# Scaling the sample states on ScalarE and adding a PSUM bank at once, in a PE-bound decoder step

## The chip, the cores and the metric

One Trainium2 chip, one of its cores. The metric is the device time of one launch in microseconds (us). Each run comes with a profile of one execution: a page of sums and a trace of every instruction. PE is TensorE's matmul side, PEld its weight loads, DVE is VectorE, ACT is ScalarE, POOL is GpSimd, SP is the sync engine, which here only issues DMAs.

## The reference

One inference step of a two-layer hybrid decoder trunk with D_MODEL = 1024: a prompt of 512 tokens, and 8 samples of 4 tokens each that continue from stored states. Layer 0 has an mLSTM/GLA mixer and an MLP, layer 1 a Mamba-2 SSD mixer and an MLP. The change is in the SSD mixer, and there in what becomes of the samples' states. Cut to that:

```python
def _ssd_chunk(h0, inp):
    x, Bm, Cm, dt, a = inp                      # L = 4 tokens for a sample
    cs = jnp.cumsum(a, axis=1)
    ...
    y = y + jnp.einsum('btgn,bgrpn->btgrp', Cm, h0) * jnp.exp(cs)[..., None]
    csL = cs[:, -1]
    wL = jnp.exp(csL[:, None] - cs) * dt
    h = jnp.exp(csL)[..., None, None] * h0 + jnp.einsum('bsgr,bsgrp,bsgn->bgrpn', wL, x, Bm)
    return h, y
```

So each sample's new state h is the old one h0 times a decay for each of 32 heads, plus a product of x and Bm. There are 4 groups of 8 heads, head dimension 64, state dimension 128: for a group and a sample the state is 512 rows by 128.

## The kernel before, in words

Everything is float32; each dense product is made of three matmuls in a reduced form of float32 (high by high, high by low, low by high), 128x128 weights against 272 tokens, at L367. The tokens (512 + 32 = 544) are taken in two halves.

TensorE's order is written out by hand. The dense matmuls are its main stream. Every other piece of work is a generator in a lane (`launch(gen, lane)`): `dense` calls `tick()` before each of its matmuls, a lane counts such ticks down, and at zero its generator runs on to its next `yield n`, where n is the ticks to wait from there. `need(key)` makes a lane wait until another has marked that key as ready. The order on the other engines is made by a planner from priorities (order in the program, with some instructions raised) and its own estimate of times. Each engine, and each engine's DMA queue with it, then runs its own list in order: an instruction that waits holds what stands behind it. ScalarE (`S`), GpSimd (`G`) and SP (`nc.sync`) issue DMAs.

PSUM has three banks for the dense products (`psd`), four for everything else (`pm(...)`, called by the name of what is put in) and one kept for the samples' outputs (`it`).

The SSD stage goes over the four groups. For a group it runs the dense products of x, B and C, each followed by a convolution over time: ScalarE copies the PSUM bank into `ci` (L1472, L1475, L1477), VectorE runs the three taps `acc` (L1487), and so on. Then `group(g, Bf, Cf)` is launched, which goes over four blocks b of 128 prompt tokens and a fifth of the 32 sample tokens: `scores(b)` loads the cumulated decays from two small DRAM tensors, `d_cs` into `E` (L1524) and, for b = 1, 2, 3, `d_ecs` (their exponentials, written at L1431) into `ec` (L1529), transposes x (`xt`, L1532) and multiplies C by B (`cb`, L1534); `state(b)` updates the prompt's state `hT`; `outputs(b)` makes the outputs. `ec` has two buffers.

When a group is done it launches `samples(g, ...)` in a lane of its own: four steps of two samples (q = 0, 2, 4, 6). A step asks for the old states twice, as `h0` (transposed, for the outputs `it`, four buffers of one sample) and as `h0n` (`hn`, two buffers of two samples, 512 KB each, L1633), makes the masked `Bm` on ScalarE (L1636), and yields. Then come the matmuls: `it` (L1640) and four products into two `sps` banks (L1647). VectorE scales a 128x128 piece of the old state by its decay and adds the product from PSUM in one operation (L1653, eight in a step, four for each bank). GpSimd's queue stores the new states from the same buffer (L1654). There are 4 groups x 4 steps = 16 steps.

The weights come through `WeightStream`: a DMA into `wraw` (three buffers), a cast on ScalarE (`whi`, L166) and the rest on VectorE (`wlo`, L167), with five sets of buffers ahead of TensorE. After its convolutions a group is gated: `zt` (L1666, L1669) and its squares.

Of the kernel before, what the change touches and what calls it, by code (L numbers as in the profile page):

```python
# [9 lines left out]
F32 = mybir.dt.float32  # L10
# [3 lines left out]
ALU = mybir.AluOpType  # L14
# [3 lines left out]
P = 128  # L18
# [3 lines left out]
NB, LS = 8, 4  # L22
# [12 lines left out]
W = dict(dec=12, gates=30, gr=8, sc=16, lev=14, v=24, kd=10, out=38, ss=40, end=12, c0=20, u=13, s=16, ml=12, mr=40, dt=238, sg=72, sx=14, sq=26, so=48, l0=12, l1=12, v0=74, v1=55, f0=16, f1=18)  # L35
# [192 lines left out]
def trunk_kernel(ctx, tc, a, stages=("ab", "mlp0", "ssd", "mlp1")):  # L228
    nc = tc.nc
    V, S, G, TE = nc.vector, nc.scalar, nc.gpsimd, nc.tensor  # L230
# [6 lines left out]
    def pm(name):  # L237
        turn[0] += 1
        k = spare[0] and turn[0] % 5 == 0
        return psm.tile([P, 512], F32, tag="k" if k else "m", name=name, bufs=1 if k else 4)  # L240
# [10 lines left out]
    for st in stages:  # L251
# [10 lines left out]
        else:  # L262
# [3 lines left out]
            for kind, m, *r in MLP:  # L266
                if kind == "pair":
                    ws.plan(st, "pair", a["mlp_w1"][l, m], a["mlp_w1"][l, m + 1])
                else:
                    k, n = m % 8, r[0]  # L270
# [53 lines left out]
    def need(*keys):  # L324
        while not ready.issuperset(keys):
            yield 0
# [1029 lines left out]
    def ssd(pool, ypool, dram, right, ahead, consts):  # L1356
# [21 lines left out]
        decs = pool.tile([P, 16, NB], F32, name="decs", bufs=1)  # L1378
        d_cs = dram.tile([32, T], F32, name="d_cs")
        d_ecs = dram.tile([32, T], F32, name="d_ecs")  # L1380
# [118 lines left out]
        def group(g, Bf, Cf):  # L1499
# [6 lines left out]
            p = pm("Btp")  # L1506
# [3 lines left out]
            p = pm("Bts")  # L1510
# [4 lines left out]
            def scores(b):  # L1515

                n = P if b < 4 else NS
                tk = slice(b * P, b * P + n)
                if b < 4:
                    E = tls[b] = pool.tile([P, 8, P], F32, tag="E", name="E", bufs=2)  # L1520
                else:
                    tls[b] = pool.tile([P, 8, NS], F32, tag="E4", name="E4", bufs=1)
                    E = tls[b][:NS]
                S.dma_start(out=E, in_=d_cs[heads, tk][None].broadcast_to([n, 8, n]))  # L1524
                ec = None
                if b in (1, 2, 3):
                    ec = pool.tile([P, 4, P], F32, tag="ec", name="ec", bufs=2)
                    for e in range(2):
                        S.dma_start(out=ec[64 * e:64 * e + 64], in_=d_ecs[8 * g + e:8 * g + 8:2, tk][None].broadcast_to([64, 4, n]))  # L1529
                p = pm("xt")  # L1530
                for j in range(4):
                    TE.transpose(p[:n, j * P:(j + 1) * P], X[:, j, tk], ident)  # L1532
                c = pm("cb")
                TE.matmul(c[:n, :n], Bf[:, tk], Cf[:, tk], start=True, stop=True)  # L1534
                if b < 4:
                    z = pool.tile([P, 512], F32, tag="z", name="z", bufs=2)
                else:
                    z = pool.tile([P, 512], F32, tag="z4", name="z4", bufs=1)
                    G.memset(z[NS:2 * NS], 0.0)
                xw = pool.tile([P, 512], F32, tag="xw", name="xw", bufs=2)  # L1540
                for o, k in ((z, 0), (xw, 32)):
                    V.tensor_tensor(o[:n].rearrange("p (h c) -> p h c", h=8), p[:n].rearrange("p (h c) -> p h c", h=8),
                                    cols[:n, b, k + 8 * g:k + 8 + 8 * g, None].broadcast_to([n, 8, 64]), ALU.mult)
                cb = pool.tile([P, P], F32, tag="cb", name="cb", bufs=1)
                if b < 4:
                    S.copy(cb, c[:, :P])
                    G.affine_select(out=E, in_=E, pattern=[[0, 8], [1, P]], compare_op=ALU.is_ge, fill=-BIG,
                                    base=0, channel_multiplier=-1)
                else:
                    V.tensor_tensor(cb[:n, :n], c[:n, :n], smask[:NS], ALU.mult)  # L1550
                    V.tensor_tensor(E, E, csp[:, heads, None].broadcast_to([n, 8, n]), ALU.min)
                for r in range(8):
                    S.activation(E[:, r], E[:, r], AF.Exp, bias=ncs[:n, b, 8 * g + r:8 * g + r + 1])
                V.tensor_tensor(E, E, cb[:n, None, :n].broadcast_to([n, 8, n]), ALU.mult)
                if b == 4:
                    G.memset(tls[b][NS:2 * NS], 0.0)
                    G.tensor_copy(tls[b][64:], seye[64:, None, :].broadcast_to([64, 8, NS]))
                tls[b] = tls[b], ec, z, xw

            def state(b):  # L1560

                E, ec, z, xw = tls[b]
                tk = slice(b * P, b * P + P)
                hT = states[0]
                if b > 0:
                    ip = pm("ip")
                    for j in range(4):
                        TE.matmul(ip[:, j * P:(j + 1) * P], hT[:, j * P:(j + 1) * P], Cf[:, tk], start=True, stop=True)  # L1568
                    V.tensor_tensor(ec, ec, ip.rearrange("p (j t) -> p j t", j=4), ALU.mult)
                sp = pm("sp")  # L1570
                TE.matmul(sp, Bt[:, b], xw, start=True, stop=True)  # L1571
                hn = pool.tile([P, 512], F32, tag="hT", name="hT", bufs=2)
                if b == 0:
                    S.copy(hn, sp)
                else:
                    G.tensor_tensor(hn.rearrange("p (h c) -> p h c", h=8), hT.rearrange("p (h c) -> p h c", h=8),
                                    dec[:, heads, b:b + 1].broadcast_to([P, 8, 64]), ALU.mult)
                    V.tensor_tensor(hn, hn, sp, ALU.add)
                states[0] = hn
                if b == 3:  # L1580
                    nc.sync.dma_start(out=a["p_h"][g], in_=hn)
# [20 lines left out]
            for b in range(4):  # L1602
                state(b)
                yield W["sx"]
                if b == 3 and g > 0:
                    yield from need(("Y", g - 1))
                scores(b + 1)
                yield W["sx"]
                outputs(b)
                yield W["sx"]  # L1610
# [10 lines left out]
            S.copy(Cm.rearrange("p (q r) -> p q r", r=NS + LS)[:, :, :LS], Cf[:, NP:].rearrange("p (q l) -> p q l", l=LS))  # L1621
            launch(samples(g, X, outputs, tls[4][2], Bs, Xs), "smp")

        def samples(g, X, outputs, z, Bs, Xs):

            heads = slice(8 * g, 8 * g + 8)
            it = psm.tile([P, 512], F32, tag="k", name="it", bufs=1)
            for q in range(0, NB, 2):
                h0 = [pool.tile([P, 512], F32, tag="h0", name="h0", bufs=4) for _ in range(2)]
                for k in range(2):  # L1630
                    nc.sync.dma_start(out=h0[k], in_=a["h0"][g, q + k])
                hn = pool.tile([P, 2, 512], F32, tag="h0n", name="h0n", bufs=2)
                nc.sync.dma_start(out=hn, in_=a["h0n"][g, q // 2])  # L1633
                Bm = pool.tile([96, 2, P], F32R, tag="Bm", name="Bm", bufs=2)
                for k in range(2):
                    S.activation(Bm[:, k], Bs.bitcast(F32), AF.Identity, scale=seqm[:96, q + k:q + k + 1])  # L1636
                yield W["sq"]

                for k in range(2):
                    TE.matmul(it[64 + NS * k:64 + NS * k + NS], Cm[:, NS * (q + k):NS * (q + k) + NS], h0[k],  # L1640
                              start=q == 0, stop=q == NB - 2)
                for i in range(2):
                    sp = pm("sps")
                    spv = sp.rearrange("p (j k n) -> p j k n", j=2, k=2)
                    for j in range(2):
                        m = 2 * i + j
                        TE.matmul(sp[:, 256 * j:256 * j + 256], Xs[:, m * P:(m + 1) * P], Bm.rearrange("p k n -> p (k n)"),  # L1647
                                  start=True, stop=True)
                    for j in range(2):
                        m = 2 * i + j  # L1650
                        for k in range(2):
                            h = hn[:, k, m * P:(m + 1) * P]
                            V.scalar_tensor_tensor(h, h, decs[:, 4 * g + m, q + k:q + k + 1], spv[:, j, k], ALU.mult, ALU.add)  # L1653
                nc.gpsimd.dma_start(out=a["s_h"][g, q // 2], in_=hn)  # L1654
            V.tensor_tensor(z[64:].rearrange("p (h c) -> p h c", h=8), it[64:].rearrange("p (h c) -> p h c", h=8),
                            ecs[64:, heads, None].broadcast_to([64, 8, 64]), ALU.mult)
            yield W["so"]
            outputs(4)
            ready.add(("Y", g))
# [163 lines left out]
    n = 0  # L1823
    spill, ahead = a["xT"], None
    left = ctx.enter_context(ExitStack())
    while n < len(stages):
        st = stages[n]
        src = spill
        with ExitStack() as stk:
            if st == "ssd":  # L1830
# [5 lines left out]
                with tc.tile_pool(name="ssd", bufs=1, reuse_waits="tile") as pool:  # L1836
# [4 lines left out]
                    with tc.manual_schedule(engines={mybir.EngineType.PE}):  # L1841
                        out = ssd(pool, ypool, dram, right, ahead, consts)
# [170 lines left out]
```

## Time and profile before

| what | value |
|---|---|
| median of 3 runs | 1509.25 us (1504.87 to 1512.08) |
| the profiled execution's own time | 1500.13 us |
| its span, first to last instruction | 1498.4 us |
| PE busy | 1471.6 us, 98% of the span |
| PEld busy | 1422.7 us, 95% |
| DVE busy | 1095.3 us, 73% |
| ACT busy | 794.1 us, 53% |
| POOL busy | 227.8 us, 15% |
| mean granted TensorE clock | 0.998 |

The page gives sums over the whole execution; an engine at 73% of the span can be full in one stage. The stretch that the change touches lies between about 660 and 1000 us of the span. A line of a waits view has who waited, for whom, then the total in us, the number of waits and the longest. A line of a timeline has the start in us, the length in us, engine, line, operation, what is written and read, the shape, and in brackets the engine's idle time before it and what ended that. "ACTq" or "SPq" is an engine's queue, where it issues a DMA; the length is that of the issue, not of the transfer.

### The profile page before, as it was taken

The numbers are of one execution on the slowest core, as the hardware profiler recorded it, in microseconds if no ns is written. First come the engines' busy times: TensorE is split into PE (matmuls) and PEld (weight loads), VectorE is DVE, ScalarE is ACT, GpSimd is POOL, SyncE is SP. The second block draws the span as 40 slices with busy tenths as digits, with TensorE's granted clock in tenths as the row PEclk, the third lists the DMA queues.
The fourth block names the chain that finished last, engine by engine and source line by source line (L and its number), as shares of the span: only waits on it lengthen the run. The fifth ranks groups of instructions, "written<-read, shape, count | busy, mean of one in ns | idle before, by whom it ended". The sixth has DMA issues, their size and how long they took to land.

```text
span 1498.4 us, 29214 instructions
## 1 busy us (share of the span) xinstructions
PE 1471.6 (98%) x11637; PEld 1422.7 (95%) x11637; DVE 1095.3 (73%) x2067; ACT 794.1 (53%) x1748; POOL 227.8 (15%) x295
## 2 busy tenths in 40 slices
PE   9999999999999999999999999999999999999997
PEld 9999989999999999999888789899999999999996
DVE  4956576786776766678898988776588677676656
ACT  6645556473543453447876676554257355444333
POOL 0511221100000000023444453420010000000000
PEclk9999999999999999999999999999999999999999
DMA  6321325223333332434466766364222233233121
GB/s 229 93 69 58 117 72 158 78 62 104 100 89 95 97 88 70 155 109 142 132 188 206 254 183 205 102 209 133 72 75 71 96 99 99 85 100 99 58 85 60
DMA packets 88369, 172.11 MB, mean 115 GB/s; under 512 B 9240, under 2 KB 43928, under 8 KB 87976
## 3 DMA queue, kind: packets, MB, share of 16 engines
q1 hardware_dynamic: 55256, 140.09, 30.2%
q10 hardware_dynamic: 30192, 19.41, 4.8%
q0 software_dynamic: 2784, 10.75, 1.8%
q8 instruction: 91, 1.49, 0.4%
q14 instruction: 46, 0.38, 0.1%
HBM read 153.48 MB, written 16.73 MB: 114 GB/s over the span
## 4 chain that ended last, share of the span: by engine, by line
PE 87%; DVE 7%; ACT 2%; DMA 2%; issue 1%; POOL 0%; ACTq 0%; SPq 0%; DVEq 0%; POOLq 0%
PE psd L367 59%; PE psd L528 18%; PE num L778 1%; PE yp L1593 1%; PE gs L1004 1%; DVE acc L1487 1%; DMA h0n<-h0n 1%; DVE wlo L167 1%; PE sp L1571 1%; DVE h0n L1653 1%; PE it L1640 1%; PE ip L1568 1%; ACT whi L166 0%; PE supd L911 0%; PE sps L1647 0%
## 5 line engine op out<-in xcount | busy, mean ns | idle before, releaser
L367 PE MATMUL psd<-xh,whi 128*128 128x272 f32 x1504 | 445.4, 296 | 2.1 <-ACT ci L1477 2.0
L367 PE MATMUL psd<-xh,wlo 128*128 128x272 f32 x1504 | 439.7, 292 | 0.0
L367 PE MATMUL psd<-xl,whi 128*128 128x272 f32 x1504 | 438.0, 291 | 0.2 <-DVE xl L287 0.2
L367 PE MATMUL psd<-hh,whi 128*128 128x272 f32 x1024 | 296.0, 289 | 0.7 <-ACT hh L286 0.7
L367 PE MATMUL psd<-hlo,whi 128*128 128x272 f32 x1024 | 295.5, 289 | 0.2
L367 PE MATMUL psd<-hh,wlo 128*128 128x272 f32 x1024 | 295.4, 288 | 0.0
L367 PEld LDWEIGHTS psd<-xh,whi 128*128 128x128 f32 x1504 | 283.5, 188 | 9.3 <-issue 5.1
L367 PEld LDWEIGHTS psd<-xl,whi 128*128 128x128 f32 x1504 | 283.8, 189 | 6.0 <-issue 4.2
L367 PEld LDWEIGHTS psd<-xh,wlo 128*128 128x128 f32 x1504 | 283.4, 188 | 4.0 <-issue 2.8
L167 DVE TENSOR_TENSOR wlo<-wraw,whi 128x1024 fp32r<-128x1024 f32 (+2 forms) x173 | 209.1, 1210 | 57.7 <-ACT whi L166 56.5
L166 ACT CAST whi<-wraw 128x1024 fp32r<-128x1024 f32 (+2 forms) x173 | 174.2, 1011 | 130.7 <-PE psd L367 115.0
L367 PEld LDWEIGHTS psd<-hh,whi 128*128 128x128 f32 x1024 | 192.8, 188 | 1.3 <-ACT hh L286 1.2
L367 PEld LDWEIGHTS psd<-hlo,whi 128*128 128x128 f32 x1024 | 192.8, 188 | 0.8 <-DVE hlo L287 0.6
L367 PEld LDWEIGHTS psd<-hh,wlo 128*128 128x128 f32 x1024 | 192.7, 188 | 0.1
L401 DVE TENSOR_TENSOR xf<-xf,psd 128x272 f32<-128x272 f32 x208 | 88.1, 433 | 77.4 <-PE psd L367 76.9
L528 PE MATMUL psd<-xh,wlo 128*128 128x272 f32 x416 | 119.9, 288 | 0.0
L528 PE MATMUL psd<-xh,whi 128*128 128x272 f32 x416 | 119.9, 288 | 0.0
L528 PE MATMUL psd<-xl,whi 128*128 128x272 f32 x416 | 119.6, 288 | 0.0
L202 ACT CAST whi<-wsum 128x1024 fp32r<-128x1024 f32 x52 | 54.3, 1044 | 111.1 <-PE psd L528 70.2
L202 ACT CAST whi<-wraw 128x1024 fp32r<-128x1024 f32 (+1 forms) x52 | 43.4, 835 | 95.4 <-PE psd L367 84.2
L203 DVE TENSOR_TENSOR wlo<-wsum,whi 128x1024 fp32r<-128x1024 f32 x52 | 63.7, 1224 | 23.3 <-ACT whi L202 23.3
L528 PEld LDWEIGHTS psd<-xl,whi 128*128 128x128 f32 x416 | 78.4, 188 | 0.0
(468 smaller groups left out, 2817.8 us busy)
## 6 DMA issues: line engine op xcount, KB each, us to landing
wraw<-mlp_w SPq DMA_DIRECT2D x80, 512.0 KB, 3.6
wraw<-ssd_in SPq DMA_DIRECT2D x40, 512.0 KB, 3.9
wraw<-mlp_w SPq DMA_DIRECT2D x64, 256.0 KB, 3.1
wraw<-ab_in SPq DMA_DIRECT2D x24, 512.0 KB, 3.7
h<-h SPq DMA_DIRECT2D x32, 256.0 KB, 3.6
h0n<-h0n SPq DMA_DIRECT2D x16, 512.0 KB, 5.5
E<-d_cs ACTq DMA_DIRECT2D x16, 512.0 KB, 5.3
s_h<-h0n POOLq DMA_DIRECT2D x16, 512.0 KB, 4.5
```

What stands on the lines that cost most here:

```text
L166: nc.scalar.copy(hi[:, r], w[:, r])
L167: nc.vector.tensor_tensor(lo[:, r], w[:, r], hi[:, r].bitcast(F32), ALU.subtract)
L202: self.cut[0] = nc.scalar.copy(hi, x).ins
L203: self.cut[1] = nc.vector.tensor_tensor(lo, x, hi.bitcast(F32), ALU.subtract).ins
L367: last[0] = TE.matmul(ps[:, :TH], wt[:, k, :], rt, start=i == 0, stop=i == n - 1).ins
L401: V.tensor_tensor(x, x, ps, ALU.add)
L528: last[0] = TE.matmul(ps, wt[:, k], bt[:, k], start=first and n == 0, stop=n == 11, skip_group_check=not first).ins
L778: TE.matmul(num[i], sT[:, i] if j == i else sT[:, (4, 7, 9)[j] + i - j - 1], vt[key][:, j, h, :w], start=j == 0, stop=j == i)
L1004: TE.matmul(p[:, 2 * m * b:2 * m * (b + 1)].rearrange("p (e t) -> p e t", e=2), z[:, 2 * m * b:2 * m * b + P], zq[:, :, m * b:m * (b + 1)] ...
L1487: V.scalar_tensor_tensor(acc[:, :n], ci[:, w:w + n], cw[:, m, w:w + 1], acc[:, :n], ALU.mult, ALU.add)
L1568: TE.matmul(ip[:, j * P:(j + 1) * P], hT[:, j * P:(j + 1) * P], Cf[:, tk], start=True, stop=True)
L1571: TE.matmul(sp, Bt[:, b], xw, start=True, stop=True)
```

## The change

It has three parts.

1. The fused scale-and-add of VectorE is taken apart. ScalarE scales the old state in its buffer (eight `S.mul` of 128x128 in a step, between the two halves of what was one yield), and VectorE adds a whole `sps` bank (128x512) in one operation: two in a step instead of eight.
2. The load of `h0n` moves into `load_old(g, q)`. The first load of a group is asked for in `group`, before `scores(4)`, and a step asks for the load of the next one. There are still two buffers.
3. The two `ec` loads of group 0, block 1 are issued by GpSimd instead of ScalarE.

```diff
                 if b in (1, 2, 3):
                     ec = pool.tile([P, 4, P], F32, tag="ec", name="ec", bufs=2)
                     for e in range(2):
-                        S.dma_start(out=ec[64 * e:64 * e + 64], in_=d_ecs[8 * g + e:8 * g + 8:2, tk][None].broadcast_to([64, 4, n]))
+                        (G if (g, b) == (0, 1) else S).dma_start(
+                            out=ec[64 * e:64 * e + 64], in_=d_ecs[8 * g + e:8 * g + 8:2, tk][None].broadcast_to([64, 4, n]))
...
                 if b == 3 and g > 0:
                     yield from need(("Y", g - 1))
+                if b == 3:
+                    load_old(g, 0)
                 scores(b + 1)
...
+        old = {}
+
+        def load_old(g, q):
+
+            old[g, q] = pool.tile([P, 2, 512], F32, tag="h0n", name="h0n", bufs=2)
+            nc.sync.dma_start(out=old[g, q], in_=a["h0n"][g, q // 2])
+
         def samples(g, X, outputs, z, Bs, Xs):
...
-                hn = pool.tile([P, 2, 512], F32, tag="h0n", name="h0n", bufs=2)
-                nc.sync.dma_start(out=hn, in_=a["h0n"][g, q // 2])
+                if q + 2 < NB:
+                    load_old(g, q + 2)
                 Bm = pool.tile([96, 2, P], F32R, tag="Bm", name="Bm", bufs=2)
                 for k in range(2):
                     S.activation(Bm[:, k], Bs.bitcast(F32), AF.Identity, scale=seqm[:96, q + k:q + k + 1])
-                yield W["sq"]
+                yield W["sq"] // 2
+                hn = old.pop((g, q))
+                for k in range(2):
+                    for m in range(4):
+                        h = hn[:, k, m * P:(m + 1) * P]
+                        S.mul(h, h, decs[:, 4 * g + m, q + k:q + k + 1])
+                yield W["sq"] - W["sq"] // 2
...
                 for i in range(2):
                     sp = pm("sps")
-                    spv = sp.rearrange("p (j k n) -> p j k n", j=2, k=2)
...
-                    for j in range(2):
-                        m = 2 * i + j
-                        for k in range(2):
-                            h = hn[:, k, m * P:(m + 1) * P]
-                            V.scalar_tensor_tensor(h, h, decs[:, 4 * g + m, q + k:q + k + 1], spv[:, j, k], ALU.mult, ALU.add)
+                    h = hn.rearrange("p k (m n) -> p m k n", m=4)[:, 2 * i:2 * i + 2]
+                    V.tensor_tensor(h, h, sp.rearrange("p (j k n) -> p j k n", j=2, k=2), ALU.add)
                 nc.gpsimd.dma_start(out=a["s_h"][g, q // 2], in_=hn)
```

`W["sq"]` is 26 ticks and `NB` is 8.

## The prediction

> **What bounds the kernel now.** I read the page first: its first part has the busy shares.
>
> ```profile
> span 1498.4 us, 29214 instructions
> ...
> PE 1471.6 (98%) x11637; PEld 1422.7 (95%) x11637; DVE 1095.3 (73%) x2067; ACT 794.1 (53%) x1748; POOL 227.8 (15%) x295
> ```
>
> The reader is to see that TensorE is busy for 98% of the span. The change adds and removes no matmul, so it can win only TensorE's idle time, 1498.4 - 1471.6 = 26.8 us over the whole kernel, and only the part of it that ends with something the change touches. Next I read the waits of TensorE, longest first. These four rows are the ones that name the decayed states (h0n, L1653) or the evacuation that stood behind the exponentials' loads (ci):
>
> ```profile
> PE xt L1532 <- DVE h0n L1653: 2.2, 1, 2.2
> PE psd L367 <- ACT ci L1477: 2.0, 1, 2.0
> ...
> PE sps L1647 <- DVE h0n L1653: 1.2, 2, 0.6
> PE cb L1534 <- DVE h0n L1653: 0.8, 1, 0.8
> ```
>
> They are five waits in all, 2.2 + 2.0 + 1.2 + 0.8 = 6.2 us, which is 0.41% of the span. That is the prize, and it is below 0.5% (7.5 us), about what a measurement of this kernel can tell from no change. Third, the busy times of the engines in the stretches where the sample states are worked on (columns: stretch, length, then PE, PEld, DVE, ACT, POOL with counts, clock, DMA share, GB/s):
>
> ```profile
> 771.00:785.00 14.00, 13.87 (x97) 10.65 (x96) 14.00 (x30) 11.33 (x32) 6.20 (x12) 1.00 0.67 221
> 840.00:856.00 16.00, 14.81 (x109) 11.85 (x110) 15.69 (x39) 9.09 (x28) 6.39 (x7) 1.00 0.86 295
> ```
>
> VectorE (the third busy time) is full in them: 14.00 of 14.00 and 15.69 of 16.00. ScalarE (the fourth) has 2.7 and 6.9 us free.
>
> **The change part by part: engine work.** Groups of instructions between 660 and 1000 us, shapes kept apart (busy us, then mean ns of one):
>
> ```profile
> L1653 DVE SCALAR_TENSOR_TENSOR h0n<-h0n,decs,sps 128x128 f32<-128x128 f32 x128 | 35.2, 340 | 5.9 <-DMA h0n<-h0n 3.6 <-PE sps L1647 2.2
> ...
> L1578 DVE TENSOR_TENSOR hT<-hT,sp 128x512 f32<-128x512 f32 x12 | 8.1, 675 | 0.0
> ...
> L1553 ACT ACTIVATE E<-E,ncs 128x128 f32<-128x128 f32 x128 | 40.1, 390 | 18.1 <-POOL E L1547 18.0
> ```
>
> Removed from VectorE: 128 fused multiply-adds, 35.2 us. Added to it: 32 adds of 128x512 with one operand in PSUM, the shape of L1578: 32 x 0.675 = 21.6 us. VectorE gains 13.6 us, 0.85 us in each of the 16 steps (four groups, four pairs of samples each). Added to ScalarE: 128 scalings of 128x128 with a per-partition scale; L1553 has that shape and took 40.1 us for 128, so 40.1 us, 2.5 us a step (0.31 us apart, 0.39 us the last). The nearest rows bound it well, so I take it. None of this lies on TensorE's path by itself; VectorE's and ScalarE's idle time covers it (403 and 704 us over the span). Where ScalarE's cover is thin, as in 771 to 785, the scalings of the first two pairs needn't lie there, since their states are loaded long before (below).
>
> **The xt and cb waits, 2.98 us.** VectorE's and TensorE's timelines where they occur (start, length; in brackets the idle time before):
>
> ```profile
> 834.40 2.14 DVE L1653 SCALAR_TENSOR_TENSOR h0n<-h0n,decs,sps 128x128 f32<-128x128 f32 x8
> 836.47 1.21 DVE L167 TENSOR_TENSOR wlo<-wraw,whi 128x1024 fp32r<-128x1024 f32 x1
> 837.60 0.43 DVE L1669 SCALAR_TENSOR_TENSOR zt<-zt,psd 128x272 f32<-128x272 f32 x1
> 837.95 0.34 DVE L1653 SCALAR_TENSOR_TENSOR h0n<-h0n,decs,sps 128x128 f32<-128x128 f32 x1
> 838.21 1.21 DVE L1492 SCALAR_TENSOR_TENSOR Cf<-Cf,acc 128x512 f32<-128x512 f32 x1
> 839.34 0.34 DVE L1653 SCALAR_TENSOR_TENSOR h0n<-h0n,decs,sps 128x128 f32<-128x128 f32 x1
> ```
> ```profile
> 837.94 0.27 PE L1511 MATMUL Bts<-scon,Bf 128*32 128x128 f32 x1
> 840.44 0.63 PE L1532 MATMUL xt<-scon,Y 128*128 128x128 f32 x4 [2.23 <-DVE h0n L1653]
> 841.82 0.35 PE L1534 MATMUL cb<-Cf,Bf 128*128 128x128 f32 x1 [0.75 <-DVE h0n L1653]
> ```
>
> The PSUM bank that xt wants holds the products of the second pair; of its four fused operations one runs at 837.95, then a Cf operation, and the next only at 839.34; xt starts at 840.44. With one add for each bank, the first pair takes 834.40 + 0.60 + 0.68 = 835.7, then wlo and zt as before bring VectorE to about 837.2, and one add ends at 837.9, before TensorE is through with Bts at 838.2. If the Cf operation (1.13 us to the next start) still goes first, the add ends at 839.0 and 0.8 us stay. Ends: 0 to 0.8 us left; I take 0.3 left, a gain of 2.7 us. The scalings of this pair can't be late: their states are asked for about 30 us earlier (SP's queue: the first two loads of this group are issued between 796.82 and 803.64).
>
> ```profile
> 796.82 6.82 SPq L1633 DMA_DIRECT2D h0n<-h0n  x2
> ```
>
> **Loading a step ahead.** That row also says what the earlier load is worth: the loads for pairs that are summed from 834.40 on have already left by 803.64, so the order in the program isn't what holds the first two pairs. What holds the third is the buffer (there are two). From the chain that ended last, in order of time:
>
> ```profile
> 778.70 4.72 DMA s_h<-h0n
> 783.44 5.70 DMA h0n<-h0n
> ```
>
> The load of the third pair starts 0.02 us after the store of the first has landed (778.70 + 4.72 = 783.42). It can't start sooner while there are two buffers; asking earlier gains nothing, and I cost the move at 0. On SP it stands ahead of two h0 loads and of weight loads; those are covered, as h0 has four buffers and the weights' stream five. If that cover were gone SP would be held from the store's issue to its landing, at most 4.7 us a step.
>
> **The sps waits, 1.2 us.** VectorE there, with the wait for the third pair's load:
>
> ```profile
> 775.53 0.59 DVE L1653 SCALAR_TENSOR_TENSOR h0n<-h0n,decs,sps 128x128 f32<-128x128 f32 x2
> 776.05 0.80 DVE L1487 SCALAR_TENSOR_TENSOR acc<-ci,sprm,acc 128x568 f32<-128x568 f32 x1
> 776.77 1.63 DVE L1653 SCALAR_TENSOR_TENSOR h0n<-h0n,decs,sps 128x128 f32<-128x128 f32 x6
> ...
> 789.27 0.61 DVE L1653 SCALAR_TENSOR_TENSOR h0n<-h0n,decs,sps 128x128 f32<-128x128 f32 x2 [2.03 <-DMA h0n<-h0n]
> 789.79 0.80 DVE L1487 SCALAR_TENSOR_TENSOR acc<-ci,sprm,acc 128x568 f32<-128x568 f32 x1
> 790.51 1.64 DVE L1653 SCALAR_TENSOR_TENSOR h0n<-h0n,decs,sps 128x128 f32<-128x128 f32 x6
> ```
>
> The first store leaves 1 us earlier (two adds and the acc end at about 777.6, not 778.4), so the third pair lands at 788.2, not 789.14. Then a bank needs six of eight scalings, 5 x 0.31 + 0.39 = 1.9 us, plus an add of 0.68: 790.8 if ScalarE is free at once; before, the bank's fourth operation ended at about 791.1 (790.51 + 0.26 to the next start + 0.34). The step saves 0.3 us and would lose as much if ScalarE is 0.6 us late. Ends: -1.2 to +1.5 us (a ScalarE late by its whole whi cast and evacuation); I take 0.
>
> **The exponentials' first loads, 2.0 us.** ScalarE's timeline (ACTq rows are DMA issues on its queue):
>
> ```profile
> 718.92 1.05 ACT L166 CAST whi<-wraw 128x1024 fp32r<-128x1024 f32 x1 [0.97 <-PE psd L367]
> 722.76 0.65 ACTq L1529 DMA_DIRECT2D ec<-d_ecs  x1
> 723.53 0.36 ACT L1475 COPY ci<-psd 128x240 f32<-128x240 f32 x1 [3.56 <-DMA d_ecs<-rows]
> ...
> 724.27 0.63 ACTq L1529 DMA_DIRECT2D ec<-d_ecs  x1
> ```
>
> ScalarE stood still for 3.56 us, from 719.97 to 723.53, because a load of ec waits, in its queue, for the write of d_ecs to land; the evacuations behind it were late and TensorE lost 2.02 us. The edit moves the two loads for block 1 of group 0 to GpSimd. But the two for block 2 (the one at 724.27 and its pair) read the same d_ecs, have a buffer of their own, stay on ScalarE, and become ready at the same landing. I expect the first of them to stand where the moved one stood: gain 0; ends 0 and 2.0 us. On GpSimd two issues of some 0.6 us each (by the rows above) are added among its own loads of the decays and its history copies; VectorE waits for nothing of GpSimd there, so 0, and 1.2 us if it did.
>
> **New waits.** ScalarE now stands in its own queue for the landing of a state; the evacuations, weight casts and exponentials queue behind it, and through the evacuations TensorE. VectorE had 3.6 us of such waits in 2 places (the L1653 group's row). At the ratio of the ec case, 2.02 us of TensorE for 3.56 us of ScalarE, they would cost 2.0 us; at neither place was an evacuation the thing TensorE waited for, so I take a quarter, 0.5 us. Ends: 0, and 8 waits (third and fourth pair, four groups) x 2.02 = 16 us. The second yield in a step shifts each step by one matmul slot (0.125 us) and adds no work: 0.
>
> **Sum.** -2.7 + 0 + 0 + 0 + 0.5 = -2.2 us. The profiled execution took 1500.13 us (span 1498.4 and 1.7 around it), which makes 1497.9. It stands 9.1 us, 0.6%, below the median of the runs, 1509.25 (1504.87 to 1512.08); laid on the median the forecast is 1507.0.
>
> **The rivals.** First, all five waits go: the planner puts another instruction than block 2's load in the slot, and ScalarE scales at once. -6.2 us, 1503.0. For it speaks that the waits are named one by one in the view; against it the load at 724.27 and the balance of the sps step.
>
> Second, the change doesn't do what it says: each add waits for the scalings and frees its bank no earlier than before. 0 us, 1509.3. For the third and fourth pairs the balance above speaks for it; for the second pair the loads issued by 803.64 speak against it.
>
> Third, on the other side: ScalarE is held by landings. Its place is the scalings of the third and fourth pairs; a planner that thinks a landing earlier than it is puts them ahead of an evacuation. Each costs 2.0 us by the ec case, eight of them 16.2, less 2.7 from xt: +13.5 us, 1522.8. It is slower by over 7.5 us from five such waits on ((7.5 + 2.7) / 2.02 = 5.05). For it: VectorE did stand for landings, twice. Against it: only twice in 16, and ScalarE has 6.9 of 16 us free at 840 to 856. [...]
>
> **How the numbers follow.** My forecast has 0.42 (range -5 to +2 us: 1504 to 1511), all five gone 0.23, no effect 0.17, ScalarE held 0.18. The range goes from 1500, all five gone and 3 us, some half of the scatter of the runs, below that, to 1517, half of the held case. No case alone reaches 7.5 us faster; of all five gone with a favourable median I give 0.12. Slower is the third rival, 0.17. The rest, 0.71, is no difference.
>
> **What would show it.** In the changed profile's waits of TensorE: xt and cb on h0n should be gone (forecast) or stay (second rival); psd on ci near 722 should stay, released by a landing of d_ecs with an ec load of block 2 in front, and be gone in the first rival; sps on h0n should be near 1 us. ScalarE should have 128 more operations of about 0.31 us, VectorE 32 of 0.67. For the third rival, idle time of ScalarE ended by "DMA h0n", with TensorE waits on ci, zt or whi just behind. The prediction is wrong if new waits of TensorE appear that name none of these tiles, since I cost the rest of the order at nothing.

## The result, and the profile after

The changed kernel is slower: 1517.74 us in the median of 20 runs (1511.29 to 1523.18) against 1508.88 (1501.20 to 1512.12) of the kernel before on the same chip, a ratio of 1.0062 [1.0050, 1.0074]. The forecast was 1507.0 and no difference, with a range that ended at 1517.

The first part of the page of the changed kernel:

```profile
span 1509.7 us, 29245 instructions
...
PE 1475.1 (98%) x11637; PEld 1425.9 (94%) x11637; DVE 1085.4 (72%) x1971; ACT 830.3 (55%) x1876; POOL 226.5 (15%) x297
```

The work moved as costed: VectorE has 96 instructions fewer and ScalarE 128 more. TensorE's busy time rose by 3.5 us although it has the same 11637 matmuls; the rest of the 11.3 us by which the span grew is idle time. So two questions: what did TensorE wait for, and why did the same matmuls take longer? The waits of TensorE, after (who waited, for whom, total, times, longest):

```profile
PE cb L1535 <- DVE Cf L1492: 4.7, 2, 4.2
PE sps L1662 <- DVE Xs L1622: 3.6, 2, 3.0
PE psd L367 <- ACT ci L1477: 3.3, 2, 2.3
...
PE psd L367 <- DVE yl L287: 1.2, 1, 1.2
```

No row names h0n any more: all four waits of before for the decayed states are gone, 4.2 us. In their place stand two that name no tile the change touches, Cf and Xs, and the ci waits have grown from one of 2.0 us to two of 3.3 in sum. Waits that name none of its tiles are what the prediction had called the sign of its being wrong. Where the 4.24 us begin, TensorE's timeline:

```profile
927.58 0.60 PE L1533 MATMUL xt<-scon,Y 128*128 128x128 f32 x4
932.43 0.80 PE L1535 MATMUL cb<-Cf,Bf 128*128 128x128 f32 x2 [4.24 <-DVE Cf L1492]
932.88 0.57 PE L367 MATMUL psd<-xh,whi 128*128 128x272 f32 x1
933.25 0.43 PE L367 MATMUL psd<-xl,whi 128*128 128x272 f32 x1
...
937.83 0.29 PE L367 MATMUL psd<-xh,wlo 128*128 128x272 f32 x1
```

Before, the same two cb matmuls waited 0.52 us:

```profile
926.20 0.49 PE L1534 MATMUL cb<-Cf,Bf 128*128 128x128 f32 x2 [0.52 <-DVE Cf L1492]
```

The rows below the wait answer the second question: the dense matmuls take 0.43 us there and start some 0.23 us apart, and from 937.8 they take 0.29 again and start 0.13 apart. VectorE made Cf late because ScalarE did. ScalarE's timeline (L1652 is the new scaling; L1490 and L1491 are the tanh at the end of a convolution, whose result VectorE completes at L1492):

```profile
920.33 2.16 ACT L1652 ACTIVATE h0n<-h0n,decs 128x128 f32<-128x128 f32 x7 [0.21 <-DMA h0n<-h0n]
922.39 0.62 ACT L1490 ACTIVATE Bf<-acc 128x512 f32<-128x512 f32 x1
922.91 0.22 ACT L1491 ACTIVATE Bf<-acc 128x32 f32<-128x32 f32 x1
923.03 0.39 ACT L1652 ACTIVATE h0n<-h0n,decs 128x128 f32<-128x128 f32 x1
...
924.63 2.46 ACT L1652 ACTIVATE h0n<-h0n,decs 128x128 f32<-128x128 f32 x8 [0.17 <-DMA h0n<-h0n]
...
930.61 0.61 ACT L1490 ACTIVATE Cf<-acc 128x512 f32<-128x512 f32 x1
```

And VectorE, which stood idle for 2.64 us until ScalarE gave it Bf:

```profile
923.04 0.69 DVE L1492 SCALAR_TENSOR_TENSOR Bf<-Bf,acc 128x512 f32<-128x512 f32 x1 [2.64 <-ACT Bf L1490]
...
931.25 1.12 DVE L1492 SCALAR_TENSOR_TENSOR Cf<-Cf,acc 128x512 f32<-128x512 f32 x1
```

These 16 scalings are those of the first two pairs of group 3. Group 3 is at its convolution of B here; its `samples` lane, and with it the sps matmuls and adds that use these states, starts only when Cf, C's convolution, is through and its blocks have run, from about 980 us on. The states were there early (ScalarE waited 0.21 and 0.17 us for their landings), and so the planner put 4.9 us of work that nobody wants for 50 us in front of Bf and Cf, which TensorE wants next. From Bf to Cf ScalarE's list now takes 8.2 us (922.39 to 930.61); before it took 3.0 (920.54 to 923.51). Busy times in the stretches (length, then PE, PEld, DVE, ACT, POOL with counts, clock, DMA share, GB/s), two of the changed kernel and then one of the kernel before:

```profile
910.00:930.00 20.00, 18.18 (x156) 17.74 (x155) 14.81 (x23) 18.16 (x54) 6.41 (x12) 1.00 0.64 216
930.00:937.00 7.00, 4.57 (x18) 4.33 (x19) 4.98 (x8) 4.12 (x15) 1.92 (x2) 0.51 0.26 75
```
```profile
910.00:930.00 20.00, 19.48 (x161) 18.43 (x160) 17.94 (x32) 13.74 (x40) 10.71 (x13) 1.00 0.71 235
```

In the first row ScalarE is busy for 18.16 of 20 us and VectorE for only 14.81; before, the same stretch had 13.74 for ScalarE, 17.94 for VectorE and 19.48 for TensorE. In the second row the granted clock is 0.51.

Matching TensorE's matmuls in the two traces gives where the 11.3 us came in. Counted as the growth of the lag of the changed kernel behind the one before:

| place | growth, us |
|---|---|
| up to 230 us, where nothing is changed: a wait of 1.4 us at 11 us, half clock behind it for 3.4 us | +1.9 |
| ci at 724 us (behind the loads of ec) and at 746 us (behind exponentials, a weight cast and a scaling in ScalarE's list, no load) | +1.3 |
| sps on Xs at 778 and 834 us, 2.98 and 0.59 us | +3.6 |
| sps, xt and cb on h0n gone, 1.2 + 2.98 us | -4.2 |
| cb on Cf at 932 us, with the half clock behind it | +5.4 |
| psd on yl at 1026 us, 1.20 us against 0.43, with the half clock behind it | +2.5 |
| all else | +0.8 |

These are two executions, one of each kernel. As the runs below show, rows of 1 to 2 us can come and go between executions with the same lists; the Cf row goes only with an edit of the list.

### The profile page after: what moved, and what is told of

Read it like the earlier page. It is cut to its first block, busy times and chain, and to the rows that moved or that the text cites. A ratio compares the mean times of both kernels' runs of the same rounds, so it can differ in the third digit from the quotient of the medians.

```text
span 1509.7 us, 29245 instructions
## 1 busy us (share of the span) xinstructions
PE 1475.1 (98%) x11637; PEld 1425.9 (94%) x11637; DVE 1085.4 (72%) x1971; ACT 830.3 (55%) x1876; POOL 226.5 (15%) x297
## 4 chain that ended last, share of the span: by engine, by line
PE 86%; DVE 6%; ACT 4%; DMA 2%; issue 1%; POOL 0%; ACTq 0%; POOLq 0%; SPq 0%; DVEq 0%
PE psd L367 58%; PE psd L528 18%; DMA E<-d_cs 1%; PE num L778 1%; DVE wlo L167 1%; PE gs L1004 1%; ACT E L1554 1%; PE it L1656 1%; PE yp L1594 1%; ACT whi L166 1%; PE sps L1662 1%; PE sp L1572 1%; PE ip L1569 0%; DMA d_ecs<-rows 0%; PE supd L911 0%
```

## The experiments

My theory after this comparison: ScalarE's scalings cost what they cost by their place in its list, above all the 16 of group 3, and a half clock behind the longer waits adds to it. The rivals: the sheer amount of work on ScalarE; the earlier loads; the ec move.

**Each part alone.** Three kernels, each the kernel before with one part of the change: the scalings and bank adds (part 1), `load_old` (part 2), the ec line (part 3).

> The kernel before with the first part alone: scalings on ScalarE, one add for each bank, the yield in two; loads and ec as before. Theory (ScalarE's order: scalings that the planner puts early stand in front of work that TensorE needs soon): most of the whole change's +0.62% is here, ratio 1.004 to 1.008, with TensorE waits on Xs near 775 us (3 us or so) or on Cf near 928 (4 us or so), and none on h0n at xt. Rival (the earlier loads move SP's and ScalarE's lists): ratio 0.996 to 1.001, no new waits.

> The kernel before with the second part alone: the load of the old states asked for a step ahead, fused operation on VectorE as before. Theory: no effect, ratio 0.998 to 1.002, waits of TensorE as before (xt on h0n 2.2 us, ci 2.0 us, sps 1.2 us). Rival (the earlier loads do it): ratio 1.003 or more.

> The kernel before with the third part alone: the two ec loads of group 0, block 1 on GpSimd. Theory: no effect, ratio 0.998 to 1.002; the wait of TensorE on ci near 722 stays at 2.0 to 2.4 us, with an ec load of block 2 where block 1's stood. Rival (the move to GpSimd disturbs the order): ratio 1.003 or more, or the wait gone and 0.998 to 0.999.

| kernel | ratio to before | median, us (before 1507.96, 35 runs) |
|---|---|---|
| part 1 alone | 1.0023 [1.0010, 1.0035] | 1512.07 |
| part 2 alone | 1.0006 [0.9993, 1.0020] | 1509.38 |
| part 3 alone | 1.0000 [0.9988, 1.0012] | 1507.36 |

Part 1 alone loses 0.23%, less than the 0.4 to 0.8% that I had expected of it. It makes the Cf wait, longer even than in the whole change, and hardly an Xs wait. The waits of TensorE with part 1 alone:

```profile
PE cb L1534 <- DVE Cf L1492: 6.8, 2, 5.8
...
PE sps L1651 <- DVE Xs L1619: 1.2, 1, 1.2
```

So the early loads are not needed for it: with the load where it was, the states of a new group's first pairs still land early. With part 2 alone the waits stand in the places of before; the one of xt on h0n is 1.3 us there and not 2.2, although in the two traces every engine but SP has the same list. Part 3 alone has the ci wait still, 2.4 us, and others than before:

```profile
PE psd L367 <- ACT ci L1477: 3.1, 2, 2.4
PE sp L1572 <- ACT cb L1547: 1.9, 1, 1.9
PE yp L1594 <- DVE ec L1570: 1.9, 2, 1.7
PE sps L1648 <- DVE Xs L1620: 1.6, 1, 1.6
```

It moves two DMA issues, but the planner's order shifts from there on (from 727 us on ScalarE), and waits on ec and Xs in group 0 stand in this trace. Its ratio is 1.0000 all the same. The three ratios add up to 1.0029, the whole is 1.0062: the parts do not add.

The complement, the changed kernel without part 3, was run too:

> The changed kernel without its third part (ec loads all on ScalarE). Theory (the loss near 928 is that of the scalings, that between 740 and 780 comes with the ec move): the waits on Xs near 775 and ci near 745 are gone, the one of cb on Cf near 928 stays at 4 us or more with a half clock behind it, ratio 1.002 to 1.0045. Rival (both losses come from the scalings): ratio 1.005 or more.

1.0037 [1.0021, 1.0053], 1513.42 us. A Cf wait of 5.0 us is there again. The Xs wait near 775 us, which I had expected to be gone, is 1.3 us. In their traces this kernel and part 1 alone have the same lists on every engine but SP, so their 1.0037 and 1.0023, whose intervals overlap, can differ only by the earlier loads. By 1.0062 and 1.0037 the ec move costs 0.25% inside the whole change, with intervals that just overlap, and nothing alone.

**Only the place of the scalings.** Two kernels keep every instruction of the change and tell the planner to issue scalings no earlier than the copy of `Xs` on ScalarE that ends their own group's preparation (a bound on the order, not a wait): all four groups, or group 3 alone.

```diff
-                S.copy(other, s_)
+                xs = S.copy(other, s_).ins
...
+                with tc.issue_after(xs):                                # all groups
+                with tc.issue_after(xs) if g == 3 else nullcontext():   # group 3 alone
                     for k in range(2):
                         for m in range(4):
                             h = hn[:, k, m * P:(m + 1) * P]
                             S.mul(h, h, decs[:, 4 * g + m, q + k:q + k + 1])
```

> The changed kernel with each group's scalings kept behind that group's last Xs cast in ScalarE's list, so that none can stand in front of it; the amount of work is the same. Theory (the place, not the amount): the waits on Xs near 775 and on Cf near 928 shrink to below 1 us, no half clock between 900 and 1000 us, ratio 0.994 to 1.000. Rival (ScalarE has too much work): the loss stays, ratio 1.003 or more, with waits on ci or h0n in place of those.

> The changed kernel with the scalings of group 3 alone kept behind that group's Xs casts; groups 0 to 2 as changed. Theory (the early scalings of group 3 stand in front of the Bf and Cf work and cost TensorE 4.2 us and a half clock behind it): the wait of cb on Cf near 928 falls below 1 us, no half clock within 10 us of it, ratio to the kernel before 1.001 to 1.004 instead of 1.0062. Rival (any place costs the same): the wait appears elsewhere, ratio 1.005 or more.

All groups: 1.0014 [1.0001, 1.0027], 1511.30 us. Group 3 alone: 1.0023 [1.0004, 1.0042], 1510.18 us (before 1506.63, 29 runs). ScalarE's timeline with group 3 alone has no scaling between 915.5 and 932 us:

```profile
922.68 0.61 ACT L1490 ACTIVATE Bf<-acc 128x512 f32<-128x512 f32 x1
...
927.35 0.63 ACT L1490 ACTIVATE Cf<-acc 128x512 f32<-128x512 f32 x1 [0.17 <-DVE acc L1487]
```

Bf to Cf takes 4.7 us instead of 8.2, the wait at 932 is gone, and with it the half clock:

```profile
910.00:930.00 20.00, 19.86 (x169) 19.41 (x169) 17.56 (x27) 16.88 (x48) 7.85 (x13) 1.00 0.81 258
930.00:937.00 7.00, 7.00 (x49) 6.23 (x48) 4.84 (x9) 6.42 (x21) 1.87 (x3) 1.00 0.16 62
```

The same amount of work on ScalarE, another place: from 1.0062 to 1.0023, intervals apart. In the traces of the two, every engine and every DMA queue has the same list up to 920.3 us, where the first of the 16 scalings stood; so nothing ahead of that place can be the reason, and this shows the main step of the theory. The wait on yl at 1026 us is 0.4 us with group 3 held back and not 1.2. With all groups held back, the list differs from 745 us on and the ratio is above the 0.994 to 1.000 that I had expected; the wait at 932 is gone too, but a like one stands in group 2, of 4.98 us. ScalarE there:

```profile
842.23 0.69 ACT L1646 ACTIVATE Bm<-Bs,scon 96x128 fp32r<-96x128 f32 x2
847.14 2.45 ACT L1554 ACTIVATE E<-E,ncs 128x128 f32<-128x128 f32 x8 [4.22 <-POOL E L1548]
...
850.35 0.62 ACT L1490 ACTIVATE Cf<-acc 128x512 f32<-128x512 f32 x1
```

Here eight exponentials that wait 4.22 us for GpSimd stand in front of Cf. It is the same fault with another holder: a wait listed ahead of Cf became TensorE's. Eight scalings of the group before are also among what stands between Bf and Cf there, and GpSimd's mask, for which the exponentials wait, begins at 846.01 when VectorE has added to a state; what the held-back scalings have to do with this I did not settle.

**The place, and the old ec line.** Group 3's scalings held back and part 3 undone:

> The same without the move of the ec loads (they stay on ScalarE). Theory (two causes: the scalings of group 3, and the new order of group 0 after the ec move): the waits on Xs and ci near 745 to 778 go too, ratio 0.996 to 1.000. Rival (ScalarE has too much work wherever it is put): ratio 1.002 or more.

0.9965 [0.9951, 0.9979], 1500.45 us: faster than both kernels. Against the 1.0037 of the complement above, whose lists are the same up to 920.6 us, this is the place of the 16 scalings again, here worth 0.7%. Against the 1.0023 of the kernel that differs from it by the ec line alone, it also says that the ec move loses inside the change, here 0.6%, intervals apart. Its waits of TensorE between 690 and 1050 us:

```profile
PE psd L367 <- ACT ci L1477: 2.4, 1, 2.4
PE sps L1662 <- DVE Xs L1621: 2.0, 1, 2.0
PE cb L1534 <- ACT hT L1574: 1.3, 1, 1.3
...
```

So the division of work is worth having, with ScalarE's 128 scalings as in the change. That excludes the rival of the sheer amount. These two pairs with the same lists up to 920 us also say how far a shorter wait in one trace can be trusted: the Xs wait near 775 us is 2.98 us in the changed kernel and 1.39 with group 3 held back, 1.3 in the complement and none here; and the complement has a wait of cb on h0n of 2.4 us at 847 us that is missing here. Waits of this size come and go with the same lists.

**The ec loads of block 2.** The prediction said that the load of block 2 would take the slot of the moved one. ScalarE's timeline of the changed kernel shows it there:

```profile
724.93 0.65 ACTq L1529 DMA_DIRECT2D ec<-d_ecs  x1
725.70 0.36 ACT L1475 COPY ci<-psd 128x240 f32<-128x240 f32 x1 [3.85 <-DMA d_ecs<-rows]
```

The test is the kernel before with both blocks' loads on GpSimd, `(G if (g, b) in ((0, 1), (0, 2)) else S).dma_start(`:

> The kernel before with the ec loads of blocks 1 and 2 of group 0 both on GpSimd. Theory (block 2's load takes the place of block 1's): the wait of TensorE on ci near 722, 2.0 to 2.4 us, goes or falls below 0.8 us. On the rest theory and rival differ: if GpSimd's queue is what upsets group 0, waits on Xs, ec or ci between 740 and 780 grow beyond those with one block moved; if it is a chance of the planner's new order, they may be anything. Ratio 0.998 to 1.003.

0.9968 [0.9953, 0.9983], 1503.87 us. The copy of ci at 722 now follows at once, behind 0.62 us; TensorE's wait there is gone (1.6 us are left at 743) and no Xs wait has come. Two more DMA issues on GpSimd are the difference between no gain and 0.3%, intervals just apart. The lists of the two kernels differ in much else too, so that the whole 0.3% is the ci wait is not shown.

Both gains together, group 3's scalings held back and both blocks' ec loads on GpSimd:

> The changed kernel with the scalings of group 3 behind its Xs casts and with the ec loads of both blocks 1 and 2 of group 0 on GpSimd. Theory (each of the two edits took away a wait of its own): the wait on ci near 722 and the one of cb on Cf near 928 are both gone, ratio 0.993 to 0.997. Rival (the gains of f2 and e7 were chances of the planner's order, and a new order brings new waits): ratio 0.998 or more.

0.9973 [0.9954, 0.9993], 1502.99 us (before 1507.14, 32 runs): the gains do not add. The waits for Cf at 932 and for ci at 722 are both gone, but two new ones have come:

```profile
PE cb L1535 <- DVE h0n L1666: 2.8, 1, 2.8
PE yp L1594 <- DVE E L1555: 2.7, 2, 1.5
```

**Scalings on GpSimd instead of ScalarE.** If ScalarE's list is the trouble, another engine might be free of it. One multiplication of 128x1024 a step, with the ec move extended to block 2 or undone:

```diff
-                for k in range(2):
-                    for m in range(4):
-                        h = hn[:, k, m * P:(m + 1) * P]
-                        S.mul(h, h, decs[:, 4 * g + m, q + k:q + k + 1])
+                h = hn.rearrange("p k (m n) -> p m k n", m=4)
+                G.tensor_tensor(h, h, decs[:, 4 * g:4 * g + 4, q:q + 2, None].broadcast_to([P, 4, 2, P]), ALU.mult)
```

> Scalings on GpSimd, one 128x1024 multiplication a step with the decays broadcast, instead of eight operations on ScalarE; loads ahead and one add for each bank as in the change; ec loads of blocks 1 and 2 on GpSimd. Theory (ScalarE's list is where the change loses): no wait of 4 us on Cf, ratio 0.993 to 0.998. Rival (any engine's list with other work in it loses the same, here GpSimd's gates and masks): ratio 1.000 or more, with waits that end on work behind GpSimd.

> As the kernel with scalings on GpSimd, but with all ec loads on ScalarE. Theory: the wait on ci near 722 stays at 2 us, the wait on Cf near 928 is below 1 us, ratio 0.996 to 1.000. Rival (other work in any list loses the same): 1.002 or more.

1.0026 [1.0013, 1.0039] and 1.0050 [1.0031, 1.0069]; no better. Both came out on the rival's side. GpSimd stood in its list for landings of states, by the view of the tile h0n 22.9 us in 8 places in the first, whose rows follow, and 33.4 in 9 in the second:

```profile
L1650 POOL TENSOR_TENSOR h0n<-h0n,decs x16: 1893/1994/2922, 733.9 to 997.8; 128x1024 f32<-128x1024 f32 x16
...
  DMA h0n<-h0n: 22.9, 8
```

GpSimd's list also holds the masks of E and a part of Y. TensorE waits 3.8 and 4.9 us for Y in these two, and 3.3 and 5.2 for Cf.

**The half clock by itself.** To see the price of a wait without any of the change, the kernel before with Cf of group 3 multiplied by 1 four times on GpSimd, which changes no value and delays Cf:

```diff
+            if g == 3:
+                for _ in range(4):
+                    G.tensor_scalar(Cf, Cf, 1.0, None, ALU.mult)
             launch(group(g, Bf, Cf), "ssd")
```

> The kernel before with Cf of group 3 multiplied by 1 four times on GpSimd before it is used, so that TensorE waits for it near 926 about as long as in the changed kernel (4 us); nothing of the change. Theory (a wait of that length is followed by a half clock): half clock for 3.4 or 6.8 us right behind the wait, mean granted clock of the runs lower than that of the kernel before by 0.001 to 0.003, time up by more than the wait: 5 to 8 us, ratio 1.003 to 1.0055. Rival (the clock has nothing to do with the waits): time up by the 3.5 us that the wait grows, clock unchanged.

1.0059 [1.0038, 1.0080], 1516.05 us. The wait came out as 7.5 us, almost twice what I had meant to make. Its row and the stretches around it:

```profile
PE cb L1534 <- POOL Cf L1775: 7.5, 1, 7.5
```
```profile
925.00:937.00 12.00, 7.84 (x64) 7.58 (x62) 9.75 (x17) 9.66 (x32) 8.48 (x8) 1.00 0.48 161
937.00:945.00 8.00, 4.62 (x20) 4.36 (x20) 1.48 (x2) 0.55 (x3) 3.25 (x2) 0.57 0.00 0
```

The wait is 7.0 us longer than before's 0.5; the time rose by 9.4 us (1516.05 - 1506.63). A stretch at half clock begins in the wait: 8.0 us at a mean of 0.57 are some 6.9 us at 0.5, of which 3.4 to 4.6 us lie behind the wait's end at 940.4. By my estimate from the granted 0.5 these cost at most half of that, 1.7 to 2.3 us, which would be most of the 2.4 us between (in the changed kernel the dense matmuls start 0.23 us apart in such a stretch and 0.13 outside). The trace shows that the half clock is there without the change. That the time rose by more than the wait is not shown: with six runs the interval of the ratio is 5.7 to 12.1 us, which holds 7.0.

## Why the prediction was wrong, step by step

**The xt and cb waits, -2.7 us: right.** Both are gone, 2.98 us by the trace of before and 2.0 by that of part 2 alone, which has the same lists but for SP's.

**Loading ahead, 0: right.** Part 2 alone is 1.0006 [0.9993, 1.0020].

**The ec loads, 0: right in the mechanism, wrong as a term of the whole.** Block 2's load took the slot, ScalarE waited 3.85 us and TensorE 2.32 (2.02 before). Alone the part is 1.0000. But I costed the rest of the order at nothing, and the move changed it: 1.0062 with it and 1.0037 without, or, with group 3 held back, 1.0023 and 0.9965. Which place in the new order costs this stays open.

**The sps waits, kept at about 1 us: wrong, to the good.** They are gone.

**The engine work: the amount right, the cover wrong. This is the step that failed.** The 128 scalings were costed at 40.1 us, "none of this lies on TensorE's path by itself; VectorE's and ScalarE's idle time covers it". They took 41.1 us. But idle time summed over the span covers nothing: the question is what stands behind a scaling in ScalarE's list. I wrote that the scalings of the first two pairs needn't lie where ScalarE's cover is thin, "since their states are loaded long before", and that is just what did it. Work whose inputs are ready early can be listed early, and 4.9 us of it went ahead of Bf and Cf, in a place where the chain from ScalarE over VectorE to TensorE had no slack: a wait of 4.24 us in place of 0.52, and 5.4 us of lag with the half clock. Moving these 16 scalings made 1.0062 into 1.0023 and 1.0037 into 0.9965. I had only looked at two stretches where VectorE is full, 771 to 785 and 840 to 856 us, and not at this one.

**New waits, 0.5 us: mis-sized.** They came to 4.24 - 0.52 on Cf, 2.98 + 0.59 on Xs and 1.20 - 0.43 on yl, 8.1 us. Of these the Cf wait is traced to the scalings by the runs that move them, and the yl wait went with it (0.4 us in both). The Xs wait in group 0 has no cause shown: there is none with part 1 alone, 1.6 us with part 3 alone, 1.3 without part 3 and 3.0 with all, but also 1.4 with the same lists as the last up to there, and none with the same as the one before it. VectorE is full there (in the changed kernel 7.93 of 8.00 us from 770 to 778) and makes Xs behind Bf and an acc; what decides how long TensorE waits I did not settle.

**The third rival, "ScalarE is held by landings", 1522.8 us: nearest by sign, not by mechanism.** ScalarE did wait 7.2 us in all for landings of h0n:

```profile
L1652 ACT ACTIVATE h0n<-h0n,decs 128x128 f32<-128x128 f32 x128 | 41.1, 393 | 7.2 <-DMA h0n<-h0n 7.2
```

But ahead of the Cf wait only 0.21 and 0.17 us of it lie. It was the work itself, of the first pairs, and not waits of the third and fourth. Nor is it that the scalings stand on ScalarE at all: the kernel with the same 128 there came out at 0.9965. So the sign of this rival came out by another way than the one it named.

**The clock, not costed at all.** I read 0.998 from the profile as full speed. In the traces of the two kernels the granted clock is 1.0 or 0.5: before, 1.00 up to 1491.5 us and 0.50 from 1492 to the end; after, 0.50 from 12.1 to 15.3, from 930.2 to 937.0, from 1029.2 to 1032.5 and from 1504 to the end, and 1.00 between these. Over the runs its mean was 0.9942 before (35 runs of the next round, mean time 1508.01 us) and 0.9921 after (20 runs, mean 1516.91). If the runs have no other values than these two, a mean of 1 - x over a time T is 2xT us at half clock: 17.4 us before and 24.0 after. By the estimate that these cost at most half of their length, that is up to 8.7 and 12.0 us. Taking them off leaves 1499.3 and 1504.9. By this estimate the 8.9 us between the means are some 5.6 us of waits and 3.3 of clock. It also gives a part of the 9.1 us that I laid on the sum without a cause: the profiled execution of before had a half clock only at its end (0.9978 in its trace), the runs had more (0.9942), which by the same estimate is at most 5.4 us.

## What to carry to other kernels

Idle time of an engine over the span doesn't cover work that goes into an in-order list: ask of each added instruction when its inputs are ready, when its result is wanted, and what will stand behind it, and hold back work that is ready long before it is wanted (here one such bound, with the same work, made 1.0037 into 0.9965). Moving one of two loads that wait for the same landing leaves the wait to the other (ScalarE waited 3.85 us behind block 2's load, 3.56 behind block 1's); moving both took it away (0.62 us were left, for an acc of VectorE). And on a kernel whose TensorE is 98% busy, a wait like those of 4.2 to 7.5 us here should be costed with the clock behind it. Before a wait of 1 to 3 us in one trace is laid to an edit, look whether it is there in a second trace with the same lists.

## What the runs showed of the hardware

A wait of TensorE can bring a stretch at half clock with it. In the changed kernel the granted clock is 0.50 from 930.2 to 937.0 us, where the wait of 4.24 us for Cf ends at 932.43, and 1.00 on both sides; the dense matmuls take 0.43 us in it and start 0.23 us apart, against 0.29 and 0.13 behind it. Three other waits of 5 us and more have one too:

| kernel | wait for Cf, us | stretch, us | mean granted clock |
|---|---|---|---|
| part 1 alone | 5.8 | 928 to 935 | 0.52 |
| all groups held back | 5.0 | 830 to 860 | 0.89, some 6.6 us at half |
| Cf delayed, nothing of the change | 7.5 | 937 to 945 | 0.57, some 6.9 us at half |

Shorter waits came out both ways. Between 700 and 760 us, where TensorE waits for ci in group 0, the mean clock is 1.00 with longest ci waits of 2.0 us (before), 2.2 (part 1 alone), 2.3 (the changed kernel, and Cf delayed) and 2.4 (group 3 held back, part 3 undone), but 0.97, some 3.6 us at half, with 2.3 (group 3 held back) and 2.7 (all groups held back). The Xs wait of 2.98 us in the changed kernel has none, while behind the wait of 2.79 us for h0n with both gains together (it ends at 852.56) the matmuls take 0.43 us and start 0.23 apart. Shorter ones yet have one behind them in the changed kernel: 0.50 from 12.1 to 15.3 us behind a wait of 1.40 that ends at 11.28, and from 1029.2 to 1032.5 behind the 1.20 on yl and 1.04 on yh that end at 1026.23 and 1027.79; yet a wait of 1.20 that ends at 230.97 has none. So these runs show no least length of a wait, and what decides is not shown.

My reading of why the runs of one kernel scatter is the same clock: over the 20 runs of the changed kernel the time falls by about 2 us for each 0.001 of mean clock, and over three sets of runs of the one before by 1.1 to 1.6, and 0.001 of 1508 us is 3.0 us at half clock, by the estimate above at most 1.5 us of time.

Last, the planner's order is a source of differences as large as the effect sought. Moving two DMA issues changed it from there on, at 727 us on ScalarE and 729 on VectorE; alone this came to a ratio of 1.0000, and inside the change to 0.25 or 0.6% of loss. A comparison of such a kernel tells of an edit together with the order that it happens to get; group 3's held-back scalings and the run with Cf delayed are the ones here whose lists are those of their partners up to the place of the edit, 920 and 927 us.
